# Another order of seven-product and eight-product pairs in the wide stages, and the gated products turned later and in other PSUM banks

## The chip, the core and the metric

The kernel runs on one core of a Trainium2 chip. The metric is the device time of one execution in microseconds, the median of three runs. TensorE multiplies, ScalarE (ACT) and VectorE (DVE) prepare operands and empty PSUM, SyncE's queue (SP) loads weights.

## The reference

One layer over 256 tokens of width 2048, in float32: a gated feed-forward (width 5632), a mixer (retention and sparse attention, from eleven projections), and a second gated feed-forward, each with an RMS norm before it, and a last norm. The change touches the two feed-forwards:

```python
def swiglu(h, w_gate, w_up, w_down):
    return (jax.nn.silu(h @ w_gate) * (h @ w_up)) @ w_down
x = x + 0.5 * swiglu(rmsnorm(x, ffn1_norm[l]), ffn1_w_gate[l], ffn1_w_up[l], ffn1_w_down[l])
```

## The kernel before

**Numbers.** Float32 operands are split in two parts that TensorE takes: `hi` (rounded by ScalarE, L269) and `lo` (the remainder, by VectorE, L275). One product is three matmuls of 128x512: hi by hi, hi by lo, lo by hi (`run_mms`, L221).

**Stages.** Each feed-forward has two parts. Part 0 has six chunks of 512 hidden columns, part 1 has five. A chunk multiplies x by the gate and the up columns: here they are called up00 to up10. After a part's chunks come its two halves of the down projection, down00 and down01, later down10 and down11; each half adds 1024 columns to x. Between the feed-forwards stand the mixer and w_out.

**Pairs and pieces.** A chunk goes through its contraction in pairs of 256 rows, one 1 MB load each (eight pairs in a chunk, twelve or ten in a down half). `wide` lays out each pair as its plan says. A pair "C" takes eight products (24 matmuls) in two pieces of 1024 columns. A pair "S" is a Strassen-like form with seven products (21 matmuls) in four pieces (6, 6, 6 and 3 matmuls); VectorE must first form four differences of the weights for it (`less`, L261, 128x512 each). The products of the S pairs go to seven banks, all but M8; the C pairs of the same chunk go to M2, M3, M4 and M8. `UP` is the plan of the chunks up01 to up10, `DOWN` that of the down halves of either part; up00 and w_out have C pairs alone. S pairs need their left operand as sums of blocks (`blocks_of`), in x (`x_for`) as in the gated products.

**Order.** The program walks the pieces by number. Before it emits the matmuls of piece i it has emitted the splits of pieces up to i+3, runs what is due at step i (`run_step`), and then emits the split of piece i+4. `hi` and `lo` have five buffers each, so piece i+4 waits until piece i-1 is multiplied. `raw` has three buffers, one for each load. Work is hung on steps with `after`; a generator goes on `yield n` steps later. Every engine takes its instructions in this order.

**The end of the S pairs.** `s_end` is the step after a stage's last S pair. There `sums_of` copies M1 (ACT, L443) and makes four sums of M1, M6, M5 and M7 (DVE, L437). `grow` adds them to x (down halves); the chunks keep them in `u`. At the chunk's last piece `ups`, and at its end `hidden`, add the C pairs' banks to them (L437) and form the gated product (silu on ACT, L512; product on DVE, L517).

**Turning.** The gated products `ht` are transposed by TensorE, in two batches (q = 0, 1) of four 128x128 transposes (L524) into bank M8. In the kernel before, that is four and seven steps into the next stage, in `hidden`. If the down plan has "S" for batch k = 2*cc+q, ACT copies the bank out (L528) and `blocks_of` makes the sums; otherwise ACT rounds it (L532) and DVE forms the remainder (L533). At the end of down11 of the first feed-forward x is turned too (`turn_x`), from step s_end+2 on in M1, M5, M6, M7, and after the end in M3, M8, M2, M4 (`turn_rest`).

Of the kernel before, what the change touches and what calls it, by code (L numbers as in the profile page):

```python
# [11 lines left out]
F32 = mybir.dt.float32  # L12
# [7 lines left out]
P = 128  # L20
# [6 lines left out]


PLAIN = "CCCCCCCC"
UP = "SSCSCCCC"  # L30
DOWN = ("SSCSCSCCCCCC", "SSCSCSCCCC")
NH = 8
NI = 16
TOPK = 64
# [15 lines left out]
def layer(ctx: ExitStack, tc: tile.TileContext, a: dict, out: bass.AP):  # L50
# [6 lines left out]
    tmp = ctx.enter_context(tc.tile_pool(name="tmp", bufs=2))  # L57
# [5 lines left out]
    def new(pool, shape, dt=F32, tag=None, bufs=None):  # L63
        count[0] += 1
        kw = {} if bufs is None else {"bufs": bufs}
        return pool.tile(shape, dt, name=f"{tag}_{count[0]}", tag=tag, **kw)
# [4 lines left out]
    def big(dt=F32, shape=(P, 4, T)):  # L71
        return new(mid, list(shape), dt, "mid")
# [9 lines left out]
    bank = {m: new(psum, [P, 512], F32, m) for m in ("M1", "M5", "M6", "M7", "M2", "M3", "M4", "M8")}  # L82
    MAP_A = {"11": "M7", "12": "M1", "21": "M6", "22": "M5"}
    MAP_B = {"11": "M2", "12": "M3", "21": "M4", "22": "M8"}
    turn = [0, 0]
# [15 lines left out]
    def after(step, fn):  # L101
        ends.setdefault(step, []).append(fn)
# [179 lines left out]
    def split_x(c, norm, xT, t=None):  # L282

        if t is None:
            t = new(one, [P, 2, 512], F32R, f"xg{c}")
        for j in range(2):
            g = gain(norm, c, j)
            S.activation(t[:, j, :T], xT[:, j], AF.Copy, scale=g)
            V.scalar_tensor_tensor(t[:, j, T:], xT[:, j], g, t[:, j, :T].bitcast(F32), op0=OP.mult, op1=OP.subtract)
        xg[c] = t  # L290
# [27 lines left out]
    def left_of(pairs):  # L318
        return lambda p, a: (s_block if isinstance(a, str) else c_block)(pairs[p], a)
# [7 lines left out]
    def x_for(c, norm, xT):  # L327

        if UP[c] == "S":
            split_x(c, norm, xT, big(F32R, (P, 2, 512)))  # L330
# [9 lines left out]
    def x_ext(c):  # L340
        if ext.get("x") is None:
            ext["x"] = new(one, [P, EXT], F32R, "ext")
        i = [p for p, k in enumerate(UP) if k == "S"].index(c)
        return ext["x"][:, i * EXT // 3:(i + 1) * EXT // 3].rearrange("p (b h n) -> p b h n", b=3, h=2)
# [88 lines left out]
    def add_x(t, d, c, v, scale):  # L433
        V.scalar_tensor_tensor(xcols(t, d, c), v, scale, xcols(t, d, c), op0=OP.mult, op1=OP.add)

    def tt(o, a, b):
        V.tensor_tensor(o, a, b, op=OP.add)  # L437

    def sums_of():

        u = {b: new(tmp, [P, 512], F32, t, n)
             for b, t, n in (("11", "s", 2), ("21", "s", 2), ("12", "e", 3), ("22", "e", 3))}
        S.activation(u["11"], bank["M1"], AF.Copy)  # L443
        tt(u["21"], u["11"], bank["M6"])
        tt(u["12"], u["21"], bank["M5"])
        tt(u["21"], u["21"], bank["M7"])
        tt(u["22"], u["21"], bank["M5"])
        return u

    def grow(d, scale, at, cmap, norm, done=None):  # L450

        start, s_end, half, end = at

        def early():
            u = sums_of()
            for b in ("11", "12", "21", "22"):
                add_x(int(b[0]) - 1, d, int(b[1]) - 1, u[b], scale)

        def ready(c):
            for t in range(2):  # L460
                add_x(t, d, c, bank[cmap[f"{t + 1}{c + 1}"]], scale)

        if s_end is not None:
            after(s_end, early)
        after(half, lambda: ready(1))
        after(end, lambda: ready(0))

        def squares_():
            for t in range(2):
                square_x(norm, t, 1024 * d, 1024)  # L470

        if norm is not None:
            after(end + 2, squares_)
# [3 lines left out]
    def ffn(which, norm, next_norm, last):  # L477
        wgu, wd = a[f"wgu{which}"], [a[f"wd{which}{j}"] for j in range(2)]
        c = 0
        for part, n in enumerate(PARTS):  # L480
            hs = {}
            marks[which, part] = len(pieces)
            for cc in range(n):
                cmap = MAP_A if c == 0 else MAP_B
                start, s_end, half, end = wide(wgu[c], PLAIN if c == 0 else UP, left_of(xg if c == 0 else xs), cmap,
                                               c == 0 and which == 1)
                u = {}

                def early(u=u):
                    u.update(sums_of())  # L490

                if s_end is not None:
                    after(s_end, early)

                def full(b, u=u, cmap=cmap):

                    if b in u:
                        tt(u[b], u[b], bank[cmap[b]])
                        return u[b]
                    return bank[cmap[b]]  # L500

                def ups(u=u, full=full):
                    for b in ("12", "22"):
                        if b in u:
                            full(b)

                def hidden(u=u, full=full, cc=cc, part=part, hs=hs, cmap=cmap):
                    ht, sil = [], []
                    for t in range(2):
                        g = full(f"{t + 1}1")  # L510
                        s = u[f"{t + 1}1"] if u else new(tmp, [P, W], F32, "s")
                        S.activation(s, g, AF.Silu, scale=r_tok[norm][:, t:t + 1])  # L512
                        sil.append(s)
                    for t in range(2):
                        b = f"{t + 1}2"
                        ht.append(u[b] if u else new(tmp, [P, W], F32, "e", 3))
                        V.scalar_tensor_tensor(ht[t], u[b] if u else bank[cmap[b]], r_tok[norm][:, t:t + 1], sil[t],  # L517
                                               op0=OP.mult, op1=OP.mult)
                    yield 4
                    for q in range(2):  # L520
                        v = bank["M8"].rearrange("p (j t) -> p j t", j=2)
                        for j in range(2):
                            for t in range(2):
                                TE.transpose(v[:, j, t * P:(t + 1) * P], ht[t][:, halves(2 * q + j, P)], ident)  # L524
                        k = 2 * cc + q
                        if DOWN[part][k] == "S":
                            f = half_k("b")
                            S.activation(f, v, AF.Copy)  # L528
                            hs[k] = blocks_of(f, big(F32R, (P, 4, 2, P)), big(F32R, (P, 3, 2, P)))
                        else:  # L530
                            h = big(F32R, (P, 2, 512))
                            S.activation(h[:, :, :T], v, AF.Copy)  # L532
                            V.tensor_tensor(h[:, :, T:], v, h[:, :, :T].bitcast(F32), op=OP.subtract)  # L533
                            hs[k] = h
                        yield 3

                after(half, ups)
                after(end, hidden)
                c += 1

            marks[which, part, "down"] = len(pieces)
            for d in range(2):
                at = wide(wd[part][d], DOWN[part], left_of(hs), MAP_B)
                start, s_end, half, end = at
                final = last and part == 1 and d == 1
                if part == 1 and d == 0:
                    after(end, lambda: act_table(AF.Sqrt))
                grow(d, 0.5, at, MAP_B, next_norm if part == 1 and not final else None)
                if final:
                    after(end, finish)  # L550
                elif part == 1 and not last:
                    if d == 0:
                        turns = list(range(4))
                    else:
                        for i, m in enumerate(("M1", "M5", "M6", "M7")):
                            after(s_end + 2 + i, lambda i=i, m=m: turn_x(i, next_norm, m))
                        turn_rest(end, next_norm)
        return end
# [403 lines left out]
    s = m_av + 1  # L962
# [8 lines left out]
    s = max(done_at["aq"] + 3, s + 20)  # L971
# [7 lines left out]
    s = done_at["rk"] + 3  # L979
# [3 lines left out]
    for g in range(2):  # L983
        h0 = 4 * g
        s = done_at["rq"] - 5 + 8 * g
# [3 lines left out]
        s = rv_end[g] + 1  # L989
# [37 lines left out]
    n = len(pieces)  # L1027
# [57 lines left out]
def _layout(i):  # L1085
# [5 lines left out]
    for w in (1, 2):  # L1091
        gu = [i[f"ffn{w}_w_{m}"][0].reshape(D, FF // W, W) for m in ("gate", "up")]
        arr[f"wgu{w}"] = _pairs(np.concatenate(gu, 2).reshape(D, 2 * FF), [PLAIN] + [UP] * (FF // W - 1))
        for j, h in enumerate(np.split(i[f"ffn{w}_w_down"][0], [PARTS[0] * W])):
            arr[f"wd{w}{j}"] = _pairs(h, [DOWN[j]] * 2)
    w = i["w_in"][0]
# [30 lines left out]
```

## Time and profile before

| | |
|---|---|
| three runs | 1951.05, 1952.14, 1955.49 us |
| profiled execution | 1953.62 us, span of its instructions 1951.8 us |
| mean granted TensorE clock | 0.991 |
| PE busy in the span | 1886.5 us (97%) |
| DVE busy | 1624.5 us (83%) |
| ACT busy | 1062.5 us (54%) |

The profiled execution stands 1.5 us above the median. A busy PE is a matmul under way, at whatever clock was granted.

### The profile page before, as it was taken

Reading aid. Unit: us, or ns where it says so; the run is one execution under the profiler, and the core shown is the slowest. Engines: PE = TensorE matmul, PEld = TensorE weight load, DVE = VectorE, ACT = ScalarE, POOL = GpSimd, SP = SyncE. Lnnn points to the kernel's source line nnn. Section 1 sums busy time; section 2 is a strip of 40 time slices with the busy share of each in tenths; the row PEclk is TensorE's granted clock in tenths of the full one; section 3 lists DMA queues with packets and bytes.
Section 4 is the critical chain, followed back from the end, with each engine's and each line's share of the span. In section 5 each row is a group of like instructions: output and inputs, shape, how many; then the busy total and the mean of one; then the engine's idle time right before and its main releaser. Section 6 shows DMA issues by size and latency. Waiting matters only on the chain.

```text
span 1951.8 us, 22696 instructions
## 1 busy us (share of the span) xinstructions
PE 1886.5 (97%) x8624; PEld 1526.5 (78%) x8624; DVE 1624.5 (83%) x2076; ACT 1062.5 (54%) x1348; POOL 5.3 (0%) x14
## 2 busy tenths in 40 slices
PE   8999999998999999999999999999999999999997
PEld 6777777876777778888888888777777887777776
DVE  7899888989998898789865656898888888999897
ACT  7555455544555455656545556555455445555554
POOL 0000000000000000000000000000000000000000
PEclk9999999999999999999999999999999999999999
DMA  8445445544445445545444545445454445545453
GB/s 324 173 173 194 173 172 212 198 154 172 173 182 198 173 181 194 184 165 212 176 144 158 182 172 205 157 191 196 178 186 172 181 186 194 193 174 187 180 194 151
DMA packets 51309, 359.33 MB, mean 184 GB/s; under 512 B 5856, under 2 KB 5856, under 8 KB 8704
## 3 DMA queue, kind: packets, MB, share of 16 engines
q1 hardware_dynamic: 50400, 355.62, 49.4%
q8 instruction: 67, 1.10, 0.2%
q10 hardware_dynamic: 432, 1.08, 0.2%
q0 software_dynamic: 368, 1.19, 0.2%
q14 instruction: 42, 0.34, 0.0%
HBM read 355.76 MB, written 2.10 MB: 183 GB/s over the span
## 4 chain that ended last, share of the span: by engine, by line
PE 74%; DVE 19%; ACT 3%; issue 2%; DMA 0%; DVEq 0%; ACTq 0%
PE M L221 58%; DVE lo L275 11%; PE M L145 8%; DVE raw L261 5%; PE M L147 4%; ACT hi L269 2%; PE M L163 1%; PE M L164 1%; PE M L162 1%; DVE mid L533 1%; DVE mid L306 0%; ACT mid L302 0%; PE M L784 0%; DVE s L437 0%; ACT sq L375 0%
## 5 line engine op out<-in xcount | busy, mean ns | idle before, releaser
L269 ACT ACTIVATE hi<-raw 128x1024 fp32r<-128x1024 f32 (+2 forms) x853 | 842.5, 1008 | 667.7 <-PE M L221 290.9
L275 DVE TENSOR_TENSOR lo<-raw,hi 128x1024 fp32r<-128x1024 f32 (+2 forms) x853 | 969.0, 1160 | 213.9 <-ACT hi L269 206.8
L221 PE MATMUL M<-hi,xg 128*128 128x512 f32 x2240 | 738.9, 398 | 18.4 <-DVE mid L533 11.6
L221 PE MATMUL M<-hi,mid 128*128 128x512 f32 x1696 | 537.0, 395 | 16.4 <-ACT hi L269 8.5
L221 PEld LDWEIGHTS M<-hi,xg 128*128 128x128 f32 x2240 | 424.8, 190 | 124.4 <-DVE mid L533 14.3
L221 PE MATMUL M<-lo,xg 128*128 128x512 f32 x1120 | 451.3, 403 | 12.8 <-DVE lo L275 11.1
L221 PEld LDWEIGHTS M<-hi,mid 128*128 128x128 f32 x1696 | 322.0, 190 | 85.9 <-DVE mid L533 9.6
L221 PE MATMUL M<-lo,mid 128*128 128x512 f32 x848 | 334.4, 394 | 3.2 <-DVE lo L275 3.2
L221 PEld LDWEIGHTS M<-lo,xg 128*128 128x128 f32 x1120 | 212.4, 190 | 84.9 <-DVE lo L275 38.8
L261 DVE TENSOR_TENSOR raw<-raw 128x512 f32<-128x512 f32 x368 | 254.5, 692 | 11.8
L145 PE MATMUL M<-xg,hi 128*128 128x512 f32 x688 | 244.9, 398 | 0.1
L221 PEld LDWEIGHTS M<-lo,mid 128*128 128x128 f32 x848 | 161.3, 190 | 41.2 <-DVE lo L275 8.5
L147 PE MATMUL M<-xg,lo 128*128 128x256 f32 x645 | 182.1, 282 | 0.0
L145 PEld LDWEIGHTS M<-xg,hi 128*128 128x128 f32 x688 | 128.3, 188 | 29.1 <-issue 1.3
L221 PE MATMUL M<-hi,ext 128*128 128x512 f32 x360 | 144.9, 404 | 1.9 <-DVE e L517 1.7
L147 PEld LDWEIGHTS M<-xg,lo 128*128 128x128 f32 x645 | 121.3, 188 | 0.8
L221 PEld LDWEIGHTS M<-hi,ext 128*128 128x128 f32 x360 | 67.8, 188 | 17.4 <-DVE e L517 2.6
L437 DVE TENSOR_TENSOR s<-s,M 128x512 f32<-128x512 f32 x96 | 65.7, 686 | 13.9 <-PE M L221 12.7
L221 PE MATMUL M<-lo,ext 128*128 128x512 f32 x180 | 71.0, 394 | 0.0
L512 ACT ACTIVATE s<-s,r_tok 128x512 f32<-128x512 f32 x40 | 28.4, 725 | 43.1 <-DVE s L437 43.1
L437 DVE TENSOR_TENSOR e<-s,M 128x512 f32<-128x512 f32 x56 | 38.5, 687 | 1.9
L221 PEld LDWEIGHTS M<-lo,ext 128*128 128x128 f32 x180 | 34.0, 189 | 6.4 <-DVE lo L275 0.2
(173 smaller groups left out, 905.1 us busy)
## 6 DMA issues: line engine op xcount, KB each, us to landing
raw<-in_wgu SPq DMA_DIRECT2D x175, 1024.0 KB, 4.8
raw<-in_wd SPq DMA_DIRECT2D x88, 1024.0 KB, 4.8
raw<-in_w_out SPq DMA_DIRECT2D x16, 1024.0 KB, 4.8
raw<-in_w_iq SPq DMA_DIRECT2D x8, 1024.0 KB, 4.8
raw<-in_w_aq SPq DMA_DIRECT2D x8, 1024.0 KB, 4.8
raw<-in_w_rk SPq DMA_DIRECT2D x8, 1024.0 KB, 4.9
raw<-in_w_rq SPq DMA_DIRECT2D x8, 1024.0 KB, 4.8
raw<-in_w_rv SPq DMA_DIRECT2D x8, 1024.0 KB, 4.8
```

Source lines behind the costliest of these rows:

```text
L145: TE.matmul(acc, lhsT=hi[:, c:c + P], rhs=r, start=st, stop=sp)
L147: TE.matmul(acc[:, T:], lhsT=lo[:, c:c + P], rhs=r[:, :T], start=False, stop=False)
L162: TE.matmul(o, lhsT=h, rhs=hi[:, i * n:(i + 1) * n], start=st, stop=False)
L163: TE.matmul(o, lhsT=h, rhs=lo[:, i * n:(i + 1) * n], start=False, stop=False)
L164: TE.matmul(o, lhsT=l, rhs=hi[:, i * n:(i + 1) * n], start=False, stop=sp)
L221: TE.matmul(bank[m], lhsT=p["left"](p["pair"], a)[u], rhs=(hi, lo)[v][:, off:off + 512], start=st, stop=sp)
L261: V.tensor_tensor(r[:, o:o + 512], r[:, a:a + 512], r[:, b:b + 512], op=OP.subtract)
L269: S.activation(hi[:, :p["n"]], raw, AF.Copy)
L275: V.tensor_tensor(lo[:, :p["n"]], raw, hi[:, :p["n"]].bitcast(F32), op=OP.subtract)
L437: V.tensor_tensor(o, a, b, op=OP.add)
L512: S.activation(s, g, AF.Silu, scale=r_tok[norm][:, t:t + 1])
L533: V.tensor_tensor(h[:, :, T:], v, h[:, :, :T].bitcast(F32), op=OP.subtract)
```

## The change

The plans keep their numbers of S pairs and put a C pair after each:

```diff
-UP = "SSCSCCCC"
-DOWN = ("SSCSCSCCCCCC", "SSCSCSCCCC")
+UP = "SCSCSCCC"
+DOWN = ("SCSCSCSCCCCC", "SCSCSCSCCC")
```

`s_end` is with this at step 16 of a chunk's 22 (before 14), and at step 22 of a down half's 32 or 28 (before 20). `sums_of` becomes a generator: at s_end it copies M1 and forms the first sum, which empties M1 and M6; at s_end+1 it runs the turning that the chunk before has left in the list `turning`; at s_end+2 it makes the other three sums. `hidden` no longer turns: it puts its two batches in that list, and `turn` writes batch 0 to M1 and batch 1 to M6.

```diff
-    def sums_of():
+    def sums_of(u):
...
+        u["11"], u["21"] = (new(tmp, [P, 512], F32, "s") for _ in range(2))
         S.activation(u["11"], bank["M1"], AF.Copy)
         tt(u["21"], u["11"], bank["M6"])
+        yield 1
+        turns = list(turning)
+        turning.clear()
+        for f, m in zip(turns, ("M1", "M6")):
+            f(m)
+        yield 1
+        u["12"], u["22"] = (new(tmp, [P, 512], F32, "e", 3) for _ in range(2))
         tt(u["12"], u["21"], bank["M5"])
         tt(u["21"], u["21"], bank["M7"])
         tt(u["22"], u["21"], bank["M5"])
...
-                    yield 4
-                    for q in range(2):
-                        v = bank["M8"].rearrange("p (j t) -> p j t", j=2)
+
+                    def turn(m, q):
+                        v = bank[m].rearrange("p (j t) -> p j t", j=2)
...
-                        yield 3
+                    turning.extend(lambda m, q=q: turn(m, q) for q in range(2))
```

`grow` and the chunks call the generator at s_end. The pairs of x that need both forms are now 0, 2 and 4 (before 0, 1 and 3), and the batches of gated products that need sums are k = 0, 2, 4, 6 (before 0, 1, 3, 5).

## Rows read from the trace of the kernel before

**Rows 1.** The page's first part: busy us, share of the span, instructions of each engine.

```profile
PE 1886.5 (97%) x8624; PEld 1526.5 (78%) x8624; DVE 1624.5 (83%) x2076; ACT 1062.5 (54%) x1348; POOL 5.3 (0%) x14
```

**Rows 2.** Waits of TensorE over the span: total, times, longest, in us.

```profile
PE M L221 <- DVE mid L533: 19.5, 10, 2.0
PE M L221 <- DVE lo L275: 14.2, 45, 1.1
```

**Rows 3.** Timeline of a stretch of the first up04: start, us, engine, line, what.

```profile
196.35 0.60 PE L524 MATMUL M<-ident,e 128*128 128x128 f32 x4
196.71 0.48 PE L221 MATMUL M<-hi,ext 128*128 128x512 f32 x1
...
201.62 3.49 DVE L275 TENSOR_TENSOR lo<-raw,hi 128x1024 fp32r<-128x1024 f32 x3
...
205.03 0.68 DVE L533 TENSOR_TENSOR mid<-M,mid 128x512 fp32r<-128x512 f32 x1
...
205.76 0.72 PE L221 MATMUL M<-hi,xg 128*128 128x512 f32 x1 [1.94 <-DVE mid L533]
```

**Rows 4.** Windows: stretch, us; busy (instructions) by engine; PEclk, DMA share, GB/s.

```profile
55.16:100.78 45.62, 44.45 (x191) 35.05 (x192) 41.38 (x56) 24.85 (x31) 0.00 (x0) 1.00 0.47 180
100.78:146.12 45.34, 44.66 (x192) 34.78 (x191) 41.52 (x53) 25.17 (x30) 0.00 (x0) 1.00 0.49 185
100.78:285.97 185.19, 179.34 (x765) 140.63 (x764) 163.51 (x197) 99.09 (x114) 0.00 (x0) 0.99 0.49 182
191.47:239.49 48.02, 45.77 (x193) 36.09 (x191) 40.31 (x47) 24.37 (x27) 0.00 (x0) 0.96 0.49 175
205.70:209.30 3.60, 3.54 (x9) 2.80 (x10) 3.50 (x6) 2.11 (x2) 0.00 (x0) 0.53 0.64 264
285.97:354.40 68.43, 66.09 (x286) 53.42 (x284) 56.72 (x65) 34.70 (x37) 0.00 (x0) 0.98 0.50 184
354.40:417.20 62.80, 62.80 (x277) 51.72 (x276) 54.06 (x61) 31.96 (x33) 0.54 (x1) 1.00 0.55 203
417.20:515.91 98.71, 90.72 (x375) 69.99 (x374) 92.54 (x122) 48.09 (x56) 0.00 (x0) 0.98 0.47 171
515.91:654.73 138.82, 135.25 (x575) 105.59 (x573) 123.36 (x151) 74.72 (x87) 0.00 (x0) 0.99 0.49 182
654.73:712.76 58.03, 55.32 (x237) 44.44 (x236) 52.34 (x63) 32.69 (x36) 0.00 (x0) 0.97 0.49 180
1285.17:1470.34 185.17, 179.30 (x765) 140.62 (x764) 163.54 (x197) 99.11 (x114) 0.00 (x0) 0.99 0.49 182
1601.53:1644.05 42.52, 42.52 (x184) 34.39 (x183) 37.49 (x43) 21.76 (x23) 0.00 (x0) 1.00 0.52 197
1644.05:1691.47 47.42, 45.20 (x193) 34.77 (x191) 43.09 (x59) 26.30 (x33) 0.00 (x0) 1.00 0.47 178
1691.47:1828.84 137.37, 133.80 (x575) 104.34 (x574) 123.26 (x151) 74.62 (x87) 0.00 (x0) 1.00 0.49 184
```

**Rows 5.** VectorE's groups in up02 of the second feed-forward: count | busy us, mean ns | idle before.

```profile
L275 DVE TENSOR_TENSOR lo<-raw,hi 128x1024 fp32r<-128x1024 f32 x19 | 22.6, 1220 | 2.4 <-ACT hi L269 2.4
L261 DVE TENSOR_TENSOR raw<-raw 128x512 f32<-128x512 f32 x12 | 8.3, 692 | 0.4
L437 DVE TENSOR_TENSOR s<-s,M 128x512 f32<-128x512 f32 x5 | 3.4, 687 | 1.4 <-PE M L221 1.4
L275 DVE TENSOR_TENSOR lo<-raw,hi 128x512 fp32r<-128x512 f32 x3 | 2.1, 687 | 0.0
```

**Rows 6.** Timelines of VectorE and ScalarE in the first up03 (146.12 to 191.47 us).

```profile
147.10 1.46 DVE L517 SCALAR_TENSOR_TENSOR e<-e,r_tok,s 128x512 f32<-128x512 f32 x2
...
181.61 1.23 DVE L275 TENSOR_TENSOR lo<-raw,hi 128x1024 fp32r<-128x1024 f32 x1 [1.57 <-ACT hi L269]
...
180.52 1.06 ACT L269 ACTIVATE hi<-raw 128x1024 fp32r<-128x1024 f32 x1 [1.73 <-PE M L221]
```

**Rows 7.** Waits of TensorE in the last down half of the first feed-forward (712.76 to 768 us).

```profile
PE M L221 <- DVE lo L275: 0.8, 1, 0.8
```

More of the change, by code (lines that the diff above doesn't have):

```diff
@@ L437, in tt @@
         V.tensor_tensor(o, a, b, op=OP.add)
-    def sums_of():
-        u = {b: new(tmp, [P, 512], F32, t, n)
-             for b, t, n in (("11", "s", 2), ("21", "s", 2), ("12", "e", 3), ("22", "e", 3))}
+    def sums_of(u):
+        u["11"], u["21"] = (new(tmp, [P, 512], F32, "s") for _ in range(2))
         S.activation(u["11"], bank["M1"], AF.Copy)
         tt(u["21"], u["11"], bank["M6"])
+        yield 1
[5 more added lines that the diff above has]
+        u["12"], u["22"] = (new(tmp, [P, 512], F32, "e", 3) for _ in range(2))
         tt(u["12"], u["21"], bank["M5"])
@@ L447, in sums_of @@
         tt(u["22"], u["21"], bank["M5"])
-        return u
+    turning = []
     def grow(d, scale, at, cmap, norm, done=None):
@@ L454, in early @@
         def early():
-            u = sums_of()
+            u = {}
+            yield from sums_of(u)
             for b in ("11", "12", "21", "22"):
@@ L487, in ffn @@
                 u = {}
-                def early(u=u):
-                    u.update(sums_of())
                 if s_end is not None:
-                    after(s_end, early)
+                    after(s_end, lambda u=u: sums_of(u))
                 def full(b, u=u, cmap=cmap):
```

## The prediction

> **What bounds the kernel now.** I read the page's busy shares first [rows 1]. TensorE is busy for 97% of the span, which leaves 65 us at most, but a matmul at a low clock counts as busy too, so the waits come next. TensorE waits longest for the remainder of a turned batch (L533: ten times, 19.5 us), then for weight remainders (L275: 45 times, 14.2 us) [rows 2]. Both are VectorE's work; what TensorE lacks is therefore either VectorE's time or a better place for it.
>
> The timeline of the first up04 shows the first kind [rows 3]. Batch 1 was turned into M8 at step 7. Its remainder (205.03) stood in VectorE's queue behind three splits, and the C pair of step 8 is the next to write M8, so TensorE waited 1.94 us. The windows then show the price [rows 4]: in the 3.6 us behind that wait the granted clock is 0.53, so nearly all of them were at 1.2 GHz, where it had been 2.4 GHz before the wait. That is another 3.6 x 0.47 = 1.7 us: 3.6 us in all for one wait. This happens where both batches belong to C pairs of the down plan; ACT frees the bank earlier for an S batch, and such chunks end in 45.3 us instead of 48.0.
>
> The second kind is VectorE's pace. From its groups in one chunk [rows 5], a full `lo` takes 22.6/19 = 1.19 us, a half one 0.7, a difference 0.69. An S pair needs 3 x 1.19 + 0.7 + 4 x 0.69 = 7.0 us of VectorE, a C pair 2.4. For TensorE I take the chunk that has no wait and no turning, 42.52 us for its 183 matmuls [rows 4]: 0.232 us each, 4.9 us for an S pair, 5.6 for a C pair. So two S pairs in a row put VectorE 14.0 - 9.8 = 4.2 us behind, right after the product work of `hidden` and beside both turned batches; and in the four C pairs at the chunk's end it idles (1.57 us at 181.61, where ACT's `hi` waits for TensorE to free a buffer [rows 6]).
>
> **The floor of a chunk.** Eight transposes cost 2 x 0.36 us (196.35 to 196.71) [rows 3], and the first matmul behind them is a little late: 0.8 us. So TensorE alone needs 42.5 + 0.8 = 43.3 us. VectorE is busy for 41.5 us in a chunk whose batches are one C and one S, 40.3 where both are C [rows 4]. TensorE stays the bound if VectorE can be nearly idle-free.
>
> **The change, part by part.** Matmuls, splits, differences, transposes and loads keep their number; only places change.
>
> *Alternation.* S then C needs 9.4 us of VectorE against 10.5 of TensorE, so no pair of pairs falls behind. I follow one chunk from its first matmul (T = 0). `hidden` holds VectorE until T = 2.4 (147.10 + 1.46 against the chunk's start at 146.12 [rows 6]). The first split behind it, piece 4, ends at 3.9, and TensorE wants it at 4.9. The S pair of pieces 6 to 9 is split from 4.9 to 11.7, where TensorE wants these pieces from 10.5 on, the last at 14.7. From there on the five buffers hold VectorE back, not its own pace: piece 16, for instance, is split when piece 11 is multiplied, 20.9 + 1.06 (ACT) + 1.2 = 23.2, and wanted at 25.8. No wait is left up to here.
>
> *The turning.* It leaves M8, so the ten waits with their slow stretches go. It now needs M1 and M6 emptied, which `sums_of` does at step 16, behind the split of piece 19. That split starts when piece 14 is multiplied, T = 25.0; ACT's `hi` 1.06, VectorE's `lo` 1.2, the sum 0.69 [rows 5, 6]: 28.0. TensorE comes to the transposes after piece 16, at 28.5. They fit with 0.5 us to spare, and I cost the new wait at nothing; behind the transposes stand all later matmuls, so if that cover goes, each microsecond is TensorE's. M1 and M6 are written again only in the next stage.
>
> *The end of the chunk.* The batches, three sums, `ups` and the next chunk's first four splits now share three C pairs. From T = 28.0 VectorE has one `lo` (1.2), the batches (0.68 for a C one; an S one's seven small operations about 1.9 instead, since busy time grows by 41.5 - 40.3), three sums (2.1), four splits with four differences (7.0), one to two us lost on ACT and on buffers, `ups` (1.4): it comes to `hidden` between T = 43.4 and 44.4. Now it begins 0.5 us before the next chunk does (its four operations take 2.9 us and end at T = 2.4), so it is about 1.0 to 1.5 us late, and the split of piece 4, which now ends 1.0 us before TensorE wants it, about 0.4 us late. I take 43.8 us for a chunk that follows one with an S batch, and 43.5 for the others. Bounds: below 43.3 (TensorE alone), above 45.3 (VectorE keeps the idle time of 3.8 us that it has in such a chunk now).
>
> *Other places.* The pairs of x with two forms move by one place; that work lies in up00 and w_out, where nothing waits for it (and costs something only if it were wanted within one or two steps; it is wanted some seven steps later). In down10, batch k = 8 is turned at step 23 and multiplied at step 24. Between lie 12 matmuls, 2.7 us, against ACT's rounding (no longer than a full `hi`, 1.06) and VectorE's remainder (0.68): covered by about 1 us. At the end of down11 of the first feed-forward, sums and four additions to x now fall on step 24, where `turn_x` begins and wants M5 two operations early: I charge 1.5 us, between nothing and 3.
>
> **The sum.** Stretches are in [rows 4].
> - up02 to up05 and up08 to up10, both times: 185.19 + 138.82 + 185.17 + 137.37 = 646.6 before, 14 x 43.8 = 613.2 after: 33.3 us.
> - up01, twice (the other within 0.01): 2 x (45.62 - 43.5) = 4.2. The second up07: 47.42 - 43.5 = 3.9.
> - down00, twice (within 0.05): the clean half takes 62.80; 62.8 + 0.8 = 63.6 against 68.43: 9.7.
> - down10: 228 of 276 matmuls are 51.9; + 0.8 + 0.4 = 53.1 against 58.03, and half a microsecond less the second time: 9.3.
> - The first up06 and up07 also carry the position tables. VectorE is busy for 92.54 of 98.71 us, so it is the bound here and half its idle time goes at most: 3.1.
> - down11, twice: a wait of 0.8 and its neighbourhood, 1.1 each, go with the adjacent S pairs [rows 7]; less the 1.5 above: 0.7.
>
> Together 64.2 us: 1953.6 - 64.2 = 1889.4 by the profiled execution. This stood 1.5 us over the median, so I predict **1888 us**.
>
> **The rivals.**
>
> *A. No lateness at all.* Every chunk at TensorE's floor of 43.3: 14 x 0.5 = 7 us more, 1881. For it: in pairs of pairs VectorE gains 1.1 us each. Against it: three C pairs hold what four held.
>
> *B. VectorE becomes the bound.* Chunks behind an S batch end at 45.0, because the idle time that VectorE needs for buffers and ACT comes back: 14 x 1.2 = 17 us less, 1905. For it: only 43.3 - 41.5 = 1.8 us of idle time are left in such a chunk. Against it: today's idle time lies in the C run, where VectorE had caught up.
>
> *C. The waits move to the new banks, and it is slower.* If the first sum comes 2.0 us after TensorE reaches the transposes, each of the 22 turnings costs what M8 costs now, 3.6 us: 79 us, so 1967. It decides from 64/22 = 2.9 us for each turning: a wait of 1.2 with the 1.7 of the low clock, so with a sum 1.7 us later than worked out. For it: the remainder behind three splits in [rows 3] is just such a lateness. The Trainium skill says the same as a rule (PSUM — Partial Sum Buffer, section Engine vs sequencer instructions): VectorE's queue is strictly first in, first out, and matmuls start and complete in program order, so a late sum stops all matmuls behind the transposes. The trace agrees with that. Against it: at that step VectorE follows TensorE's buffers, not the other way round, and it would have to be 1.7 us behind its S pair there.
>
> *D. The change does not do what it says.* The lateness is the chunk's total, not its order; the stalls shift from the first pairs to the last, or to the turnings with 1 us each. Then half or less is gained: 1920 to 1950.
>
> **How the numbers follow.** Forecast (1881 to 1898) 0.50; A (below 1881) 0.12; B (1898 to 1920) 0.20; D 0.11; C 0.07, nearly all of it above 1956. The time is the likeliest case. The range 1876 to 1920 takes in the forecast, B and most of A: 0.8. A measurement of this kernel tells 0.2%, 4 us, from no change: faster 0.92, same 0.02, slower 0.06.
>
> **What would show it.** Right: TensorE's waits for L533 are gone from its list; no chunk has a granted clock under 0.99; chunks last 43.3 to 44.3 us and VectorE is busy for 95% of them; TensorE's waits for `lo`, where any are left, sit at a chunk's fifth piece. Wrong: waits at the transposes for a sum (C); chunks still at 45 us with VectorE idle in them (B, D); a granted clock near 0.96 in chunks behind the turnings.

## The result and the profile after

Three runs beside the profiled one gave a median of 1887.75 us for the four (1887.16 to 1888.34), against 1953.82 us before (four runs): a ratio of 0.966 (95% interval 0.965 to 0.968), 66 us. The profiled execution took 1887.65 us.

The page of the changed kernel; its first line is the span, the second answers to [rows 1]:

```profile
span 1885.8 us, 22691 instructions
PE 1856.2 (98%) x8624; PEld 1527.1 (81%) x8624; DVE 1625.8 (86%) x2076; ACT 1064.9 (56%) x1348; POOL 5.3 (0%) x14
```

VectorE's work is the same to 1.3 us. Of the 66 us, 36 are time in which TensorE stood idle (65 us before, 30 now). For the other 30 us it counts as busy for less time with the same 8624 matmuls. The clock explains about 12 of these by the mean granted clock (0.991 before, 0.997 now: 0.009 x 1951.8 less 0.003 x 1885.8). The rest is not the clock: in up02, at a granted clock of 1.00 in both kernels, busy time fell from 44.66 to 43.60 us. A matmul's row there lasts 0.39 us and the next row begins 0.23 us after its start, so a short pause lies in part under a row that counts as busy. TensorE's longest waits in the changed kernel:

```profile
PE M L221 <- ACT hi L269: 7.8, 1, 7.8
PE M L221 <- DVE lo L275: 2.1, 2, 1.8
PE M L221 <- DVE e L522: 1.7, 2, 0.9
PE M L221 <- DVE e L437: 1.4, 1, 1.4
PE M L364 <- DVE e L437: 1.4, 1, 1.4
PE M L145 <- DVE xg L289: 1.1, 1, 1.1
PE M L364 <- DVE x L434: 0.8, 2, 0.5
```

The first is the start of the kernel. The waits for a turned remainder [rows 2] are gone, those for `lo` fell from 45 to 2. No line of the whole list names the new transposes (L529).

The windows of the stages, in the columns of [rows 4]: first up01, up02, then up02 to up05, down00, up06 with up07, up08 to up10, down10, down11 with the mixer; of the second feed-forward up02 to up05, up07, up08 to up10.

```profile
55.76:99.26 43.50, 43.50 (x192) 35.42 (x193) 38.92 (x48) 24.29 (x28) 0.00 (x0) 1.00 0.52 188
99.26:142.86 43.60, 43.60 (x192) 35.24 (x191) 41.57 (x53) 25.23 (x30) 0.00 (x0) 1.00 0.52 193
99.26:273.82 174.56, 174.56 (x765) 140.83 (x764) 166.26 (x205) 99.80 (x117) 0.00 (x0) 1.00 0.52 193
273.82:337.32 63.50, 63.50 (x285) 52.65 (x284) 56.79 (x65) 34.69 (x37) 0.00 (x0) 1.00 0.55 200
399.89:492.87 92.98, 89.08 (x376) 70.48 (x375) 89.68 (x114) 47.34 (x53) 0.00 (x0) 0.98 0.50 180
492.87:623.94 131.07, 131.07 (x575) 105.43 (x573) 124.66 (x157) 75.81 (x90) 0.00 (x0) 1.00 0.52 193
623.94:677.14 53.20, 53.13 (x238) 43.48 (x236) 51.11 (x61) 30.82 (x35) 0.00 (x0) 1.00 0.53 197
677.14:1070.81 393.67, 389.81 (x2197) 335.53 (x2196) 297.15 (x447) 225.93 (x340) 3.34 (x6) 1.00 0.49 174
1250.97:1425.39 174.42, 174.42 (x765) 140.96 (x764) 166.28 (x205) 99.73 (x117) 0.00 (x0) 1.00 0.52 193
1593.98:1637.37 43.39, 43.39 (x193) 35.31 (x192) 40.41 (x51) 25.53 (x30) 0.00 (x0) 1.00 0.51 192
1637.37:1768.27 130.90, 130.90 (x575) 105.56 (x574) 124.72 (x157) 75.70 (x90) 0.00 (x0) 1.00 0.52 193
```

In the chunks TensorE's busy time equals the length of the stretch: it is the bound. VectorE is busy for 41.57 of 43.60 us in up02, the same 41.5 that lay in 45.34 us before.

The place where the change could have gone wrong is the turning. The timelines of the changed up04, which begins at 186.47 us: ScalarE's copy of M1, VectorE's first sum, the eight transposes.

```profile
212.94 0.58 ACT L442 ACTIVATE s<-M 128x512 f32<-128x512 f32 x1
...
211.72 2.58 DVE L275 TENSOR_TENSOR lo<-raw,hi 128x1024 fp32r<-128x1024 f32 x2 [0.16 <-ACT hi L269]
214.22 0.68 DVE L437 TENSOR_TENSOR s<-s,M 128x512 f32<-128x512 f32 x1
...
215.26 1.04 PE L529 MATMUL M<-ident,e 128*128 128x128 f32 x8
216.06 0.48 PE L221 MATMUL M<-hi,xg 128*128 128x512 f32 x1
```

The sum ends at 214.90 and the transposes begin at 215.26, behind a matmul and not behind a wait. In T that is 28.4 and 28.8. All eight cost 0.80 us. The first four go into M1, which ScalarE's copy alone empties (213.52); the sum empties M6, which the second four want half of the 0.80 us later. So the cover at M6 is about 0.36 + 0.4 = 0.8 us.

### The profile page after: what moved, and what is told of

Read it like the earlier page. It is cut to its first block, busy times and chain, and to the rows that moved or that the text cites. A ratio compares the mean times of both kernels' runs of the same rounds, so it can differ in the third digit from the quotient of the medians.

```text
span 1885.8 us, 22691 instructions
## 1 busy us (share of the span) xinstructions
PE 1856.2 (98%) x8624; PEld 1527.1 (81%) x8624; DVE 1625.8 (86%) x2076; ACT 1064.9 (56%) x1348; POOL 5.3 (0%) x14
## 4 chain that ended last, share of the span: by engine, by line
PE 93%; DVE 5%; ACT 1%; issue 1%; DMA 0%; DVEq 0%; ACTq 0%
PE M L221 75%; PE M L145 8%; PE M L147 4%; DVE lo L275 2%; PE M L529 1%; PE M L163 1%; PE M L164 1%; PE M L162 1%; DVE raw L261 1%; DVE x L434 1%; ACT hi L269 1%; PE M L790 0%; DVE e L437 0%; PE M L838 0%; PE M L144 0%
## 5 line engine op out<-in xcount | busy, mean ns | idle before, releaser
L221 PE MATMUL M<-hi,mid 128*128 128x512 f32 x1696 | 531.1, 392 | 8.2 <-ACT hi L269 7.8
L221 PE MATMUL M<-lo,xg 128*128 128x512 f32 x1120 | 444.4, 397 | 2.3 <-DVE lo L275 2.1
L437 DVE TENSOR_TENSOR s<-s,M 128x512 f32<-128x512 f32 x96 | 64.1, 682 | 2.2 <-PE M L221 1.2
L704 ACT ACTIVATE b<-e 64x512 f32<-64x512 f32 (+2 forms) x46 | 28.1, 612 | 19.5 <-DVE e L690 18.9
```

The costliest lines, as they stand in the source:

```text
L221: TE.matmul(bank[m], lhsT=p["left"](p["pair"], a)[u], rhs=(hi, lo)[v][:, off:off + 512], start=st, stop=sp)
L704: S.activation(b[p0:p0 + w], q[p1:p1 + w], AF.Copy)
```

## The experiments

Each stands against the kernel before on the same chip (1953.14 us for the first four, 1955.25 us for the rest). The changed kernel was not run again beside them, and the kernel before differs by up to 2 us between chips (1953.14 to 1955.25), so a difference of that size from 1887.75 us says little.

**The turning alone.** The changed kernel with the two old plans:

```diff
-UP = "SCSCSCCC"
-DOWN = ("SCSCSCSCCCCC", "SCSCSCSCCC")
+UP = "SSCSCCCC"
+DOWN = ("SSCSCSCCCCCC", "SSCSCSCCCC")
```

> The changed kernel with the two old plans: only the turning moves to M1 and M6 behind the S pairs, two S pairs still stand together. My theory (two separate causes, the late remainder in M8 and VectorE's 4.2 us of arrears after two S pairs): the waits for L533 and the stretches at a granted clock near 0.5 go, the waits for lo at a chunk's pieces 5 and 6 stay. Worked out: behind `hidden` (T = 2.4) piece 5 is split at 7.2 and wanted at 6.3, piece 6 at 9.0 and wanted at 8.6, so about 1.3 us in each chunk, 44.7 us instead of 43.6. In all 1911 us (1903 to 1918). Rival, the turning is everything: 1888 to 1892, no waits left. Rival, the order is everything: over 1930.

Measured: 1911.73 us, ratio 0.979 (0.978 to 0.981). Its waits of TensorE:

```profile
PE M L221 <- DVE lo L275: 20.7, 46, 1.1
PE M L221 <- ACT hi L269: 9.2, 4, 8.2
```

The window of its up02:

```profile
99.75:144.45 44.70, 43.92 (x193) 35.14 (x191) 41.45 (x53) 25.07 (x30) 0.00 (x0) 1.00 0.50 188
```

The waits for a turned remainder are gone and those for `lo` all there (46 of them, before 45); the chunk takes 44.70 us where 44.7 was worked out. So the causes are two. The turning is worth 1953.14 - 1911.73 = 41.4 us of the gain, and the order 1911.73 - 1887.75 = 24.0 once the turning is moved. Neither rival holds. What the order is worth with the old turning was not run.

**The old order in the chunks alone.** The changed kernel with `UP = "SSCSCCCC"`.

> The changed kernel with the old plan in the chunks alone; the down halves keep their alternation. My theory: the 17 chunks with S pairs of their own and an ordinary start get the waits for lo back, about 1.1 us each, so 1887.8 + 18 = 1906 us, and the down halves stay as in the changed kernel (63.5 and 53.2 us). If the order is worth nothing once the turning is moved: 1888. If the order in the down halves is what counts: within 4 us of 1888 too, and the kernel with both old plans far above it.

Measured: 1905.05 us, ratio 0.976 (0.974 to 0.977). That is within 1 us of the 1906 expected. The order in the chunks is worth 1905.05 - 1887.75 = 17.3 us, that in the down halves 1911.73 - 1905.05 = 6.7 (beside the old order in the chunks; the down plans also say which batches need sums).

**The bank alone.** The kernel before, with the batch copied out of M8 first:

```diff
+                            f = half_k("b")
+                            S.activation(f, v, AF.Copy)
-                            S.activation(h[:, :, :T], v, AF.Copy)
-                            V.tensor_tensor(h[:, :, T:], v, h[:, :, :T].bitcast(F32), op=OP.subtract)
+                            S.activation(h[:, :, :T], f, AF.Copy)
+                            V.tensor_tensor(h[:, :, T:], f, h[:, :, :T].bitcast(F32), op=OP.subtract)
```

> The kernel before with one edit: for a C batch too, ScalarE copies M8 out whole, and rounding and remainder are made from that copy, so that the bank no longer waits for VectorE. Order and place of the turning stay. My theory: the ten waits of 1.9 us for L533 and the low clock behind them go, the waits for lo stay; chunks of 48.0 and 46.5 us fall to about 45.2, down00 and down10 by 3.4 each, 26 us in all: 1928 us (1922 to 1934). If the turning's place in VectorE's queue matters and not the bank: over 1945. If the bank's wait is the whole gain: near 1890.

Measured: 1937.32 us, ratio 0.992 (0.991 to 0.994): 15.8 us, not 26, and outside the range that was expected. The windows of its up02 and up04:

```profile
102.10:148.07 45.97, 44.86 (x192) 34.77 (x191) 41.65 (x53) 25.80 (x31) 0.00 (x0) 1.00 0.48 184
194.06:239.38 45.32, 44.46 (x192) 34.92 (x191) 40.10 (x47) 25.30 (x29) 0.00 (x0) 1.00 0.50 186
```

Where the wait of 1.94 us had been, in up04, the chunk fell from 48.02 to 45.32 us as expected, and the clock is back at 1.00. But up02, which had no such wait, grew from 45.34 to 45.97. ScalarE's timeline in that up02, around the two copies out of M8:

```profile
110.65 0.58 ACT L533 ACTIVATE b<-M 128x512 f32<-128x512 f32 x1
111.26 0.63 ACT L534 ACTIVATE mid<-b 128x512 fp32r<-128x512 f32 x1
111.80 2.94 ACT L269 ACTIVATE hi<-raw 128x1024 fp32r<-128x1024 f32 x3
114.64 0.57 ACT L528 ACTIVATE b<-M 128x512 f32<-128x512 f32 x1
```

The second copy stands behind three splits in ScalarE's queue as well, and the added operation pushes it back: it starts 12.5 us after the chunk's beginning, in the kernel before 11.9 (112.65 in the chunk that begins at 100.78). The chunk is longer by as much. Freeing the bank by another engine is thus only part of a cure while the bank is wanted at step 8 (15.8 us, where the other place gave 41.4): ScalarE has splits ahead of it as well. The traces of the two kernels, stage by stage, account for the miss: the ten stages that had a wait for L533 are 23.1 us shorter together, the eight chunks that turn one batch of either kind and had no such wait are 5.2 us longer (0.55 to 0.72 each), the second up07 is 0.9 longer and the start, up to up01, 1.3. Together that is 15.7.

**The turning one step earlier.** The changed kernel without the first `yield 1` of `sums_of`, so that TensorE comes to the transposes before M1 and M6 are empty. The three later sums come a step earlier with it.

> The changed kernel with the turning one step earlier, right behind the first sum (step 16 instead of 17 of a chunk), so that TensorE wants M6 before VectorE has emptied it. My theory has the first sum end at T = 28.0 and TensorE come to the transposes at 25.7: a wait of about 2.3 us at each of 22 turnings, and behind it up to 1.7 us for the low clock, as behind the 1.94 us wait of before: 51 to 88 us more than the changed kernel, 1938 to 1976. If the sum has more room than worked out, and the step makes no difference: 1888.

Measured: 1940.27 us, ratio 0.994 (0.992 to 0.995), 52.5 us above the changed kernel or 2.4 for each turning. Its waits of TensorE:

```profile
PE M L528 <- ACT s L442: 20.7, 22, 1.0
PE M L528 <- DVE s L437: 15.7, 22, 0.7
```

(20.7 + 15.7)/22 = 1.65 us for each turning, shorter than the 2.3 worked out. The list also shows that there are two waits and not one: the four transposes into M1 wait for ScalarE's copy (L442), the four into M6 for the sum (L437). Behind them comes the low clock, in part of the places. The timeline at the turnings in up02 and up03:

```profile
130.45 0.66 PE L528 MATMUL M<-ident,e 128*128 128x128 f32 x4 [0.94 <-ACT s L442]
131.82 0.66 PE L528 MATMUL M<-ident,e 128*128 128x128 f32 x4 [0.72 <-DVE s L437]
...
175.94 0.66 PE L528 MATMUL M<-ident,e 128*128 128x128 f32 x4 [0.93 <-ACT s L442]
177.31 0.98 PE L528 MATMUL M<-ident,e 128*128 128x128 f32 x4 [0.72 <-DVE s L437]
```

The windows behind each of the two:

```profile
132.20:135.60 3.40, 3.40 (x18) 2.78 (x17) 3.06 (x8) 2.56 (x5) 0.00 (x0) 1.00 0.90 357
177.70:181.10 3.40, 3.40 (x11) 2.77 (x10) 3.07 (x8) 2.23 (x4) 0.00 (x0) 0.53 0.90 354
```

This is rival C of the prediction, made to happen: one step in the place of the turning takes back four fifths of the gain.

**One bank instead of two.** Batch 0 is turned into M1 at s_end+1, batch 1 into M1 a step later:

```diff
-        for f, m in zip(turns, ("M1", "M6")):
-            f(m)
-        yield 1
+        for f in turns:
+            f("M1")
+            yield 1
+        if not turns:
+            yield 1
```

> The changed kernel with one bank in place of two: batch 0 is turned into M1 at step s_end+1, batch 1 into M1 too, one step later. If what counts is that the turning stands in the run of C pairs, where the bank has a whole piece of 2.8 us to be emptied before it is written again (copy 0.6, remainder 0.7 or seven small operations of about 1.9 us), one bank does: 1886 to 1890 us and no wait at the transposes. If it takes two banks: each of 22 second batches waits 1 to 2 us for the remainder of the first, 1910 to 1960.

Measured: 1891.45 us, ratio 0.968 (0.966 to 0.969), 3.7 us above the changed kernel's median. That is 1.5 us above the range that was expected. No wait at the transposes of gated products is in its list. So it is not the second bank that pays, but the place, with a bank (M1) that nothing else wants before the next stage. One wait is new there:

```profile
PE M L221 <- DVE x L434: 2.8, 2, 1.4
```

It stands in the down11 of either feed-forward (the first time between 679 and 690 us, at its start): sums and additions to x fall a step later in down10 than in the changed kernel, and a matmul there waits for one of VectorE's additions to x.

**The position tables spread.** The changed kernel with the tables begun in down01, every third step; the second kernel also makes all four sums at once where nothing is to be turned (`if turning:` around the two yields and the turning). The cut shows one of the yields; all those between the tables' operations change alike.

```diff
-        yield 1
+        yield 3
...
-    after(marks[1, 1] + 2, lambda: tables(marks[1, 1, "down"] + 2))
+    after(marks[1, 1] - 27, lambda: tables(marks[1, 1, "down"] + 2))
```

> The changed kernel with the position tables begun 27 steps before up06 (in down01) instead of 2 steps behind its start, and with three steps between two of their operations instead of one. My theory: up06 and up07 of the first feed-forward are now the one place where VectorE is the bound (46.9 + 46.0 us where the second feed-forward takes 42.5 + 43.4). VectorE's 12 us of tables fit in the idle time of down01 (8.7 us) and up06 (5 us), if spread. Of the 7.0 us at stake 3 to 6 come back: 1882 to 1885. If down01 has no idle time at the right places, its S pairs wait instead: 1886 to 1890.

> As the run with the tables begun earlier, and sums_of makes its four sums at once where nothing is to be turned, so that M5 and M7 come free at step s_end for turn_x. My theory: the waits of the transposes of x for the sums at the end of down11 (1.4 us) and what follows them there go, 1.5 to 3 us below the run with the tables alone. If they come from the additions to x and not from the two steps: the same as that run.

Measured: 1880.65 us, ratio 0.962 (0.961 to 0.963), and 1879.20 us, ratio 0.961 (0.960 to 0.963). The windows of down01, up06 and up07 with the tables spread:

```profile
337.73:400.29 62.56, 62.56 (x277) 51.80 (x276) 60.17 (x75) 32.20 (x33) 0.54 (x1) 1.00 0.55 203
400.29:442.83 42.54, 42.54 (x185) 34.49 (x184) 42.13 (x50) 22.22 (x23) 0.00 (x0) 1.00 0.54 198
442.83:486.22 43.39, 43.39 (x193) 35.30 (x192) 40.39 (x51) 25.44 (x30) 0.00 (x0) 1.00 0.53 194
```

All of the 7 us come back, more than the 3 to 6 expected: VectorE is busy for 60.17 of 62.56 us and then 42.13 of 42.54, and TensorE waits for nothing. The second edit takes off 1.45 us more, just short of the 1.5 to 3 expected, and the wait for a sum at the transposes of x (1.4 us) is no longer in its list.

## Why the prediction was right

It said 1888 us and the median was 1887.75. The mechanism held; that the number agrees so closely is in part luck, as the terms below show. Its steps:

- *The 14 chunks*: 174.56 + 131.07 + 174.42 + 130.90 = 610.95 us, 43.6 each, worked out as 43.8. The gain is 35.6 where 33.3 stood.
- *up01 and the second up07*: 43.50 and 43.39, worked out as 43.5. *down00*: 63.50 against 63.6. *down10*: 53.20 against 53.1.
- *up06 and up07* (first): 92.98, worked out as 95.6. Its idle time fell from 6.2 to 3.3 us, about the half that was taken; but only 89.68 us of VectorE's work lie in the stretch now, 2.9 less than before, the rest beside other stages. Here two of the signs were missed: the granted clock is 0.98 over the two (0.96 in up06), and they take 46.9 and 46.0 us. Spreading the tables removed both.
- *down11*: this term had the wrong sign. Down11 with the mixer took 390.15 us before and takes 393.67 after: 3.5 us lost. Its new waits stand at the end of down11 and the start of the mixer: 1.4 us of the transposes of x for a sum, 0.8 for additions to x, 1.1 for xg. In the second feed-forward 65.42 became 64.56. Together 2.7 us lost where 0.7 gained was written; the mechanism was named, but its price of 1.5 us was too low: set against the 1.1 us of gain that was counted for the same place, the 3.5 us are a price of 4.6, outside the stated bounds of nothing and 3. Making the sums at once took back 1.45 us; where the rest comes from was not tried.

The errors of the three terms largely cancel: +2.3, +2.6, -3.4 (measured gain less the written one). The whole sum, 64.2 us, was 1.8 short of the 66.0 between the profiled executions (1953.62 and 1887.65). The 1.5 us that the prediction then took off, because the profiled execution stood above the median of three, made up for that. This correction had no ground: with the fourth run the median before is 1953.82, above the profiled execution. So the agreement to a quarter of a microsecond is luck; the agreement of the terms is not.

*The two mechanisms* were told apart by the first two experiments: the turning in M8, with its waits and the low clock behind them, 41.4 us; two S pairs in a row, 24 beside the moved turning. Of the ten waits with "their slow stretches" only seven had one: three stages with the same wait of 1.9 us kept a granted clock of 1.00.

*The new wait* at M6 was costed at nothing with 0.5 us to spare. The cover was about 0.8 there, because the first four transposes need only ScalarE's copy, and the run one step earlier shows that the cover mattered.

*The end of the chunk*: VectorE was expected about 0.4 us late at the fifth piece of chunks behind an S batch, hence 43.8. Each of the 14 chunks shows just this: in the changed kernel's trace, 5.2 us after the chunk's start, a weight load of the fifth piece waits 0.3 to 0.4 us for `lo`. In up02, from the weight loads' own timeline:

```profile
104.47 0.19 PEld L221 LDWEIGHTS M<-lo,xg 128*128 128x128 f32 x1 [0.37 <-DVE lo L275]
```

TensorE loses only about 0.2 us by it: the chunks take 43.6, the second up07, which has no such wait, 43.39. So the lateness is real, against rival A, and its price was put too high; 43.6 lies between A's 43.3 and the forecast, nearer the forecast. B and D are refuted by stretches in which TensorE is busy throughout, C by the waits' list. One step of the walk through the chunk is off by its own figures, without effect: piece 5 is split by 3.9 + 1.2 = 5.1, not 4.9.

## What to carry to other kernels

Work that empties a bank belongs where the bank is next wanted late, not where it first becomes possible: count what stands ahead of it in its engine's queue, and compare with the step at which TensorE comes back. Stages that cost the helper engine more than TensorE should alternate with those that cost it less, as long as the buffers between them hold only a few pieces. And look for the one stretch that carries work the others do not, as the tables here: spread over its neighbours' idle time, it cost TensorE nothing that its waits show.

## What the runs showed of the hardware

With the turning one step early, TensorE waited 0.94 + 0.72 us at the turning in up02 and 0.93 + 0.72 us in up03, behind the same kind of matmuls. After the first the granted clock stayed at 1.00 (2.4 GHz), after the second it was 0.53 over 3.4 us (most of it at 1.2 GHz), and the chunks took 45.50 and 47.06 us. Of the 22 turnings ten were followed by a granted clock of 0.50 to 0.62, twelve by 1.00. The kernel before shows the same. Seven of its ten stages with a wait for L533 have a granted clock of 0.96 to 0.98, three have 1.00. Up05 of the first feed-forward waited 1.9 us as up04 did, and took 46.48 us where up04 took 48.02 [rows 4]:

```profile
239.49:285.97 46.48, 44.24 (x192) 34.95 (x191) 40.23 (x47) 24.37 (x27) 0.00 (x0) 1.00 0.50 182
```

A wait of such a length thus has two prices, about 1.6 us apart, and here only a run told how many pay the higher.
